# A decoder trunk on one core: held sums copied into PSUM ahead of the last down-projection block, in place of additions after it

## The chip, the core and the metric

The kernel runs on one core of one Trainium2 chip. The metric is device time in microseconds, the median of several runs: 1820.44 us for the kernel before (three runs, 1819.75 to 1821.89). A profile of one execution shows five engines: TensorE (PE, with its weight loads as a row of their own, PEld), VectorE (DVE), ScalarE (ACT), GpSimd (POOL) and SyncE (SP), which starts the transfers.

## What is computed

Two layers of a hybrid decoder, on 512 rows of width 1024, all in float32. Each layer runs a DeltaNet branch and a sliding-window attention branch, merges and projects them (`w_o`), and then an MLP. The part that matters here is the end of a layer:

```python
    x = x + rmsnorm(mix, post_mix_g)

    h2 = rmsnorm(x, pre_mlp_g)
    ff = jnp.square(jax.nn.relu(h2 @ w_ff1)) @ w_ff2
    return x + rmsnorm(ff, post_mlp_g)
```

`ff` is 512 x 1024 and sums over 4096 inner columns. After it come the mean square of each row, a scaling by `post_mlp_g`, the residual sum, and for the first layer the next layer's norm and projection.

## The kernel before

Each float32 product is made of three matmuls: both operands are split into a high part (`h`, rounded to a TensorE format) and a low part (`l`, the rest), and high x high, high x low and low x high go into the same PSUM bank. A weight block `wr` of 128x1024 comes by DMA, ScalarE casts it to `wh` (L384), and VectorE makes `wl` = `wr` - `wh` (L385). Four such pairs are held at once (`LOOK`), and a cast is placed four blocks ahead of its use.

The inner dimension of the MLP goes in four blocks of 1024. The first three down blocks use a Strassen-like scheme with seven products, and their sums are held in eight SBUF tiles `acc[t][n]`: t is one of four row tiles of 128 rows, n one of two column halves of 512. The fourth block (`s = 3`) is plain:

- `ff1` (L1455) makes the last 1024 inner columns in four pairs of units. Each pair uses the banks `ps_a`, `ps_y`, `ps_z` and `ps_q`, 256 columns of each. The two last products of a pair go into `ps_y` and `ps_z`.
- `mm_b4` (L437) makes the first column half of all four row tiles together: for each of four weight blocks j, for each row tile t, six matmuls of 128x512 into the bank `ps_b` of that tile. All four tiles so end within the last block, one after another. Then, for each tile (L1638 to L1641), VectorE adds the held sum `acc[t][0]` to the bank (into SBUF), ScalarE takes the mean square of the sum (L506, `jk`, a junk output with an accumulated row sum), and VectorE multiplies it by the gain.
- `last_tiles` (L424, first layer) makes the second column half, `ps_f`: row tile 0, then 1, with 24 matmuls each, then 2 and 3 in turns of two k. After tile 0, tile 1 and the pair it calls `post_tiles` (L545): VectorE adds the held sum `acc[t][1]` (L560), ScalarE takes its mean square (L506), VectorE multiplies by the gain (L565), joins the mean squares (L511), GpSimd makes the power -1/2 (L512), and VectorE scales both halves and adds the residual (L568, L569). Then come the next layer's mean squares (L506), GpSimd's root, its scaling into `xs` (L521), and TensorE transposes `xs` into banks `ps_n` (L532, eight small matmuls for a row tile, in four-by-four), from which ScalarE and VectorE take the high and low parts (L537, L538). The transposes of tiles 0 and 1 stand between the matmuls of tiles 2 and 3 and those of tiles 2 and 3 between the next layer's first matmuls. In the last layer a plain loop (L1651) makes tile after tile, and the end of `post_tiles` stores to the output.

The eight PSUM banks are dealt to pools: `PM` (two), `PS` (three), `PK` (one), `PZ` (two). In the kernel before, `mm_b4` gets two of `PZ` and two of `PS` (`four(1)`), and `last_tiles` three turns of `PM` and `PK`.

The same function `last_tiles` is used for `w_o` earlier in the layer, where nothing is held: there ScalarE's mean square (L506) and VectorE's gain (L565, and L1366 after `mm_b4`) read the PSUM banks `ps_wo` and `ps_b` directly.

A scheduler sets the order of each engine's instructions outside the stretches that `Order` pins to the order of writing. TensorE's order at the places named here is that of the code. Engines run their queues in order.

Of the kernel before, what the change touches and what calls it, by code (L numbers as in the profile page):

```python
# [15 lines left out]
ALU = mybir.AluOpType  # L16
# [7 lines left out]
NT = S // P  # L24
KT = D // P
# [102 lines left out]
def hybrid_trunk(ctx, tc, x, positions, pre_mix_g, dn_conv_w, dn_a_log, dn_dt_bias, dn_norm_g,  # L128
# [286 lines left out]
    def mm_b(ps, ws, aT, t, ks=range(KT)):  # L415
        tsl = slice(t * P, (t + 1) * P)
        for k in ks:
            hi, lo = aT[k]
            wh, wl = ws[k // 2]
            mm(ps, lhsT=hi[:, tsl], rhs=wh[:, k % 2, :], start=k == 0, stop=False)  # L420
            mm(ps, lhsT=hi[:, tsl], rhs=wl[:, k % 2, :], start=False, stop=False)
            mm(ps, lhsT=lo[:, tsl], rhs=wh[:, k % 2, :], start=False, stop=k == KT - 1)

    def last_tiles(ws, aT, name, done, turn):  # L424

        pss = [PM(name), PM(name), PM(name), PK(name)]
        for t in range(2):
            mm_b(pss[t], ws, aT, t)
            done((t,), pss[t:])
        for k in range(0, KT, 2):  # L430
            for t in (2, 3):
                mm_b(pss[t], ws, aT, t, range(k, k + 2))
            if k in (0, 4):
                turn(k // 4)
        done((2, 3), pss[2:])

    def mm_b4(pss, aT, then=lambda: None):  # L437

        for j in range(4):
            if j == 2:  # L440
                then()
            wh, wl = weights()
            for t in range(NT):
                tsl = slice(t * P, (t + 1) * P)
                for r in range(2):
                    hi, lo = aT[j * 2 + r]
                    k = j * 2 + r
                    mm(pss[t], lhsT=hi[:, tsl], rhs=wh[:, r, :], start=k == 0, stop=False)  # L448
                    mm(pss[t], lhsT=hi[:, tsl], rhs=wl[:, r, :], start=False, stop=False)  # L449
                    mm(pss[t], lhsT=lo[:, tsl], rhs=wh[:, r, :], start=False, stop=k == KT - 1)  # L450

    def mm_c(pss, left, onto=False, js=range(2)):

# [24 lines left out]
    def four(i):  # L478
        return [b("ps_b4") for b in ((PZ, PZ, PS, PS) if i % 2 else (PM, PM, PK, PS))]
# [22 lines left out]
    def meansq(src, name):  # L502

        jk = T[4]("jk", BF16)
        q_ = sm.tile([P, 1], F32, name=name, bufs=5)
        act(out=jk, in_=src, func=AF.Square, scale=D ** -0.5, accum_out=q_)  # L506
        return q_
# [37 lines left out]
    def post_tiles(tiles, a0g, ps1, add1, q0, gb, xsrc, xdst, gb2=None, Tx=(T[5], T[6], T[7])):  # L545
# [12 lines left out]
        if add1 is not None:  # L558
            for i, t in enumerate(tiles):
                tt(out=add1[t], in0=a[i], in1=add1[t], op=ALU.add)  # L560
                a[i] = add1[t]
        q1 = [meansq(a[i], "pq1") for i in n]
        r = []
        for i, t in enumerate(tiles):
            tt(out=xo[i][:, 512:], in0=a[i], in1=gb[:, 512:], op=ALU.mult)  # L565
            r.append(rstd("pr", q0[t], q1[i]))
        for i, t in enumerate(tiles):
            stt(out=xo[i][:, :512], in0=a0g[t], scalar=r[i], in1=xt[i][0], op0=ALU.mult, op1=ALU.add)  # L568
# [26 lines left out]
    for l in range(depth):  # L595
# [778 lines left out]
            dma(xd[t * P:(t + 1) * P, :], xo)  # L1374

        def wo_tail(tiles, pss):
            xs.extend(post_tiles(tiles, m0, pss, None, s0, gb1, x_res, keep, gb2))

        last_tiles(ws, mT, "ps_wo", wo_tail, lambda t: norm_turn(xs[t], t, q2))

# [30 lines left out]
                dma(out[t * P:(t + 1) * P, i * 512:(i + 1) * 512], xo[:, i * 512:(i + 1) * 512])  # L1411

        def ff2_tail(tiles, pss):
            a0, a1 = [a[0] for a in acc], [a[1] for a in acc]
            Tx = T[0], T[3], T[6]
            if l == depth - 1:
                post_tiles(tiles, a0, pss, a1, s0, gb3, xd, give, None, Tx)
            else:
                xs_next.extend(post_tiles(tiles, a0, pss, a1, s0, gb3, xd, keep, nxt[0], Tx))
# [101 lines left out]
        for s in range(3):  # L1521
# [30 lines left out]
            def done(ms, ps):  # L1552
                if len(ms) == 2:
                    raw[ms[0] // 4] = ps
                else:
                    m, = ms
                    if m in (0, 2, 4, 6):
                        raw[m // 4] = X4("raw")
                    r_ = raw[m // 4].rearrange("p (a k n) -> p a k n", a=2, k=2)[:, :, m % 2, :]
                    act(out=r_, in_=ps.rearrange("p (a n) -> p a n", a=2), func=AF.Relu)  # L1560
                    act(out=r_, in_=r_, func=AF.Square)
                count[0] += len(ms)
                if count[0] % 4 == 0:
                    lefts(*raw)
# [68 lines left out]
                      *(a.rearrange("p (a n) -> p a n", a=2) for a in h3[m]))  # L1633

        ff1(done, pending)
        pss = four(1)
        mm_b4(pss, h3)
        for t in range(NT):  # L1638
            tt(out=acc[t][0], in0=pss[t], in1=acc[t][0], op=ALU.add)
            s0[t] = meansq(acc[t][0], "pq0")  # L1640
            tt(out=acc[t][0], in0=acc[t][0], in1=gb3[:, :512], op=ALU.mult)  # L1641
        ws = [weights() for _ in range(4)]
        if l < depth - 1:
            nxt = pre_begin(l + 1)
            xs_next = []
            order = Order(nc.tensor)
            order.begin()
            last_tiles(ws, h3, "ps_f2", ff2_tail, lambda t: norm_turn(xs_next[t], t, nxt[1]))
# [31 lines left out]
```

## Time and profile before

| what | value |
| --- | --- |
| median of three runs | 1820.44 us (1819.75 to 1821.89) |
| the profiled execution's own time | 1820.0 us |
| its span, first to last instruction | 1818.3 us |
| TensorE busy | 1796.3 us, 99% |
| VectorE busy | 1386.4 us, 76% |
| ScalarE busy | 994.9 us, 55% |
| TensorE clock, mean | 0.999 |

A row of the timeline reads: start in us from the span's start, duration in us, engine, line, operation, output <- input with shapes, how many instructions are merged, and in brackets how long the engine had been idle and whose result ended that. Matmuls overlap in their pipeline: a matmul of 128x512 lasts 0.39 us in the records, but the next starts 0.23 us after it.

### The profile page before, as it was taken

Reading aid. Unit: us, or ns where it says so; the run is one execution under the profiler, and the core shown is the slowest. Engines: PE = TensorE matmul, PEld = TensorE weight load, DVE = VectorE, ACT = ScalarE, POOL = GpSimd, SP = SyncE. Lnnn points to the kernel's source line nnn. Section 1 sums busy time; section 2 is a strip of 40 time slices with the busy share of each in tenths; the row PEclk is TensorE's granted clock in tenths of the full one; section 3 lists DMA queues with packets and bytes.
Section 4 is the critical chain, followed back from the end, with each engine's and each line's share of the span. In section 5 each row is a group of like instructions: output and inputs, shape, how many; then the busy total and the mean of one; then the engine's idle time right before and its main releaser. Section 6 shows DMA issues by size and latency. Waiting matters only on the chain.

```text
span 1818.3 us, 28382 instructions
## 1 busy us (share of the span) xinstructions
PE 1796.3 (99%) x10252; PEld 1524.3 (84%) x10252; DVE 1386.4 (76%) x2606; ACT 994.9 (55%) x2031; POOL 209.4 (12%) x386
## 2 busy tenths in 40 slices
PE   9999999999999999999999999999999999999998
PEld 8878878888788888989898887888877888889896
DVE  5499796887666878898556997968875669798974
ACT  6678742444434656566457877234443347566562
POOL 0322102221101000000012221022111010000000
PEclk9999999999999999999999999999999999999999
DMA  6633447654463244554445344585545533554551
GB/s 201 203 111 121 111 145 226 180 170 152 117 200 136 82 162 153 174 182 146 166 155 180 105 128 110 168 230 157 166 140 153 172 116 105 175 166 158 174 176 57
DMA packets 146431, 278.60 MB, mean 153 GB/s; under 512 B 33569, under 2 KB 66657, under 8 KB 146290
## 3 DMA queue, kind: packets, MB, share of 16 engines
q1 hardware_dynamic: 145778, 276.75, 48.9%
q8 instruction: 81, 1.33, 0.3%
q14 instruction: 60, 0.49, 0.1%
q0 software_dynamic: 512, 0.03, 0.0%
HBM read 239.38 MB, written 37.36 MB: 152 GB/s over the span
## 4 chain that ended last, share of the span: by engine, by line
PE 82%; DVE 5%; ACT 5%; DMA 4%; issue 1%; POOL 1%; SPq 1%; DVEq 0%; POOLq 0%; ACTq 0%
PE ps_b L449 3%; PE ps_b L448 3%; PE ps_b L450 3%; PE ps_f L400 2%; PE ps_f L401 2%; PE ps_f L402 2%; PE ps_us L400 2%; PE ps_us L401 2%; PE ps_us L402 2%; PE ps_ud L401 2%; PE ps_ud L402 1%; PE ps_ud L400 1%; PE ps_vp L402 1%; PE ps_vp L400 1%; PE ps_vp L401 1%
## 5 line engine op out<-in xcount | busy, mean ns | idle before, releaser
L384 ACT CAST wh<-wr 128x1024 fp32r<-128x1024 f32 (+2 forms) x368 | 372.5, 1019 | 439.5 <-PE ps_vp L401 59.0
L385 DVE TENSOR_TENSOR wl<-wr,wh 128x1024 fp32r<-128x1024 f32 (+2 forms) x368 | 435.2, 1191 | 177.6 <-ACT wh L384 174.4
L512 POOL TENSOR_TENSOR pr<-pq,pw 128x1 f32<-128x1 f32 x16 | 9.8, 612 | 793.4 <-DVE pq L511 793.4
L448 PE MATMUL ps_b<-wh,h_h 128*128 128x432 f32 (+1 forms) x192 | 71.1, 370 | 0.0
L449 PE MATMUL ps_b<-wl,h_h 128*128 128x432 f32 (+1 forms) x192 | 70.5, 367 | 0.1
L450 PE MATMUL ps_b<-wh,h_l 128*128 128x432 f32 (+1 forms) x192 | 70.3, 366 | 0.0
L400 PE MATMUL ps_f<-g_h,wh 128*128 128x512 f32 x160 | 62.4, 390 | 0.0
L401 PE MATMUL ps_f<-g_l,wh 128*128 128x512 f32 x160 | 62.4, 390 | 0.0
L402 PE MATMUL ps_f<-g_h,wl 128*128 128x512 f32 x160 | 62.2, 389 | 0.0
L401 PE MATMUL ps_qp<-h_l,wh 128*128 128x512 f32 x128 | 54.0, 422 | 0.0
L400 PE MATMUL ps_vp<-h_h,wh 128*128 128x512 f32 x128 | 53.7, 420 | 0.0
L402 PE MATMUL ps_vp<-h_h,wl 128*128 128x512 f32 x128 | 53.7, 419 | 0.0
L985 ACT ACTIVATE M<-M,nm 128x128 f32<-128x128 f32 x128 | 49.9, 391 | 5.9 <-DVE nm L980 5.9
L400 PE MATMUL ps_qp<-h_h,wh 128*128 128x512 f32 x128 | 51.8, 405 | 0.0
L400 PE MATMUL ps_kp<-h_h,wh 128*128 128x512 f32 x128 | 51.6, 403 | 0.0
L402 PE MATMUL ps_qp<-h_h,wl 128*128 128x512 f32 x128 | 51.4, 401 | 0.0
L401 PE MATMUL ps_vp<-h_l,wh 128*128 128x512 f32 x128 | 51.4, 401 | 0.0
L401 PE MATMUL ps_ga<-h_l,wh 128*128 128x512 f32 x128 | 51.0, 398 | 0.0
L400 PE MATMUL ps_gb<-h_h,wh 128*128 128x512 f32 x128 | 51.0, 398 | 0.0
L402 PE MATMUL ps_kp<-h_h,wl 128*128 128x512 f32 x128 | 50.9, 398 | 0.0
L402 PE MATMUL ps_ga<-h_h,wl 128*128 128x512 f32 x128 | 50.7, 396 | 0.0
L343 DVE TENSOR_TENSOR wr<-wr 128x512 f32<-128x512 f32 x72 | 47.4, 685 | 4.3 <-DMA wr<-in_weights_dram 4.1
(432 smaller groups left out, 5922.5 us busy)
## 6 DMA issues: line engine op xcount, KB each, us to landing
wr<-in_weights_dram SPq DMA_DIRECT2D x320, 512.0 KB, 3.7
wr<-in_weights_dram SPq DMA_DIRECT2D x24, 432.0 KB, 4.7
D<-dd SPq DMA_DIRECT2D x32, 256.0 KB, 2.8
xd<-xo SPq DMA_DIRECT2D x12, 512.0 KB
xt<-xd SPq DMA_DIRECT2D x24, 256.0 KB, 4.1
D<-gd SPq DMA_DIRECT2D x16, 256.0 KB, 6.0
dd<-D SPq DMA_DIRECT2D x16, 256.0 KB, 5.9
kkd<-kk SPq DMA_DIRECT2D x16, 256.0 KB, 2.0
```

Source lines behind the costliest of these rows:

```text
L343: tt(out=o_, in0=i0, in1=i1, op=ALU.add)
L384: nc.scalar.copy(wh[:, :w], wr[:, :w])
L385: sub(out=wl[:, :w], in0=wr[:, :w], in1=wh[:, :w].bitcast(F32), op=ALU.subtract)
L400: mm(ps, lhsT=wh[:, k, :], rhs=hi, start=k == 0, stop=False)
L401: mm(ps, lhsT=wh[:, k, :], rhs=lo, start=False, stop=False)
L402: mm(ps, lhsT=wl[:, k, :], rhs=hi, start=False, stop=k == KT - 1)
L448: mm(pss[t], lhsT=hi[:, tsl], rhs=wh[:, r, :], start=k == 0, stop=False)
L449: mm(pss[t], lhsT=hi[:, tsl], rhs=wl[:, r, :], start=False, stop=False)
L450: mm(pss[t], lhsT=lo[:, tsl], rhs=wh[:, r, :], start=False, stop=k == KT - 1)
L512: ptt(out=r, in0=q1, in1=mhalf[:, 0:1], op=ALU.pow)
L985: act(out=M[:, j * P:(j + 1) * P], in_=M[:, j * P:(j + 1) * P], func=AF.Exp, bias=nm[:, j:j + 1], accum_out=den[:, j:j + 1])
```

## The change

In the plain block the bank gets the held sum first. ScalarE copies `acc[t][0]` into each of `mm_b4`'s four banks, and `acc[t][1]` into each of the second half's banks; all matmuls then add onto that (no matmul of the group has `start`). VectorE's eight additions a layer (L1639 and L560 of before) are gone, ScalarE gets eight copies of 128x512 a layer, and the mean squares and gains read the bank in place of SBUF. The banks are dealt otherwise: `mm_b4` takes `PS`, `PS`, `PZ`, `PZ`, and the second half takes `PZ`, `PZ`, `PZ`, `PS` in the first layer and `PZ` for each tile in the last, in place of `PM` and `PK`.

```diff
-    def last_tiles(ws, aT, name, done, turn):
-
-        pss = [PM(name), PM(name), PM(name), PK(name)]
-        for t in range(2):
-            mm_b(pss[t], ws, aT, t)
+    def last_tiles(ws, aT, name, done, turn, seed=None):
+
+
+        pss = [b(name) for b in ((PZ, PZ, PZ, PS) if seed else (PM, PM, PM, PK))]
+        onto = seed is not None
+        for t in range(NT):
+            if onto:
+                nc.scalar.copy(pss[t], seed[t])
+            if t == 2:
+                break
+            mm_b(pss[t], ws, aT, t, onto=onto)
             done((t,), pss[t:])
+        if onto:
+            nc.scalar.copy(pss[3], seed[3])
...
-            mm(ps, lhsT=hi[:, tsl], rhs=wh[:, k % 2, :], start=k == 0, stop=False)
...
+            mm(ps, lhsT=hi[:, tsl], rhs=wh[:, k % 2, :], start=k == 0 and not onto, stop=False,
+               skip_group_check=onto)
...
-        a = list(ps1[:len(tiles)])
-        if add1 is not None:
-            for i, t in enumerate(tiles):
-                tt(out=add1[t], in0=a[i], in1=add1[t], op=ALU.add)
-                a[i] = add1[t]
+        a = ps1[:len(tiles)]
...
-        pss = four(1)
-        mm_b4(pss, h3)
+        pss = [b("ps_b4") for b in (PS, PS, PZ, PZ)]
         for t in range(NT):
-            tt(out=acc[t][0], in0=pss[t], in1=acc[t][0], op=ALU.add)
-            s0[t] = meansq(acc[t][0], "pq0")
-            tt(out=acc[t][0], in0=acc[t][0], in1=gb3[:, :512], op=ALU.mult)
+            nc.scalar.copy(pss[t], acc[t][0])
+        mm_b4(pss, h3, onto=True)
+        for t in range(NT):
+            s0[t] = meansq(pss[t], "pq0")
+            tt(out=acc[t][0], in0=pss[t], in1=gb3[:, :512], op=ALU.mult)
...
-                ps = PM("ps_f2")
-                mm_b(ps, ws, h3, t)
+                ps = PZ("ps_f2")
+                nc.scalar.copy(ps, acc[t][1])
+                mm_b(ps, ws, h3, t, onto=True)
                 ff2_tail((t,), [ps])
```

The order of the matmuls on TensorE is not changed. Where the copies stand in ScalarE's queue is set by the scheduler. The first place is the end of `ff1`, ahead of `mm_b4` in the first layer (`ps_b_9214` to `ps_b_9217` are the banks of row tiles 0 to 3, `ps_f_9388` to `ps_f_9391` those of the second half). Before, ScalarE has there:

```order
L384 CAST wh<-wr 128x1024
L1500 ACTIVATE raw<-ps_a 128x256
L1493 COPY raw<-ps_q 128x256
L384 CAST wh<-wr 128x1024 x2
L1511 ACTIVATE raw<-raw 128x512
L1513 ACTIVATE raw<-ps_z 128x256
L384 CAST wh<-wr 128x1024
L1514 ACTIVATE raw<-raw 128x1024
L486 CAST h_h<-raw 128x512 x2
```

Now it has:

```order
L384 CAST wh<-wr 128x1024
L1510 ACTIVATE raw<-ps_a 128x256
L1503 COPY raw<-ps_q 128x256
L1648 COPY ps_b_9214<-acc 128x512
L1648 COPY ps_b_9215<-acc 128x512
L384 CAST wh<-wr 128x1024 x3
L1521 ACTIVATE raw<-raw 128x512
L1523 ACTIVATE raw<-ps_z 128x256
L1648 COPY ps_b_9217<-acc 128x512
L1524 ACTIVATE raw<-raw 128x1024
L440 COPY ps_f_9391<-acc 128x512
L500 CAST h_h<-raw 128x512 x2
```

The copies into `ps_b_9214`, `ps_b_9215`, `ps_b_9217` and `ps_f_9391` have come in (that into `ps_b_9216` stands a little earlier), and a weight cast (L384) has moved ahead of the two activations on `raw` (L1511 and L1513, which are L1521 and L1523 now).

The second place is the step from `mm_b4` to the second half, again on ScalarE in the first layer (`pq` and `nq` are the mean squares). Before:

```order
L384 CAST wh<-wr 128x1024 x3
L506 ACTIVATE jk,pq_9340<-acc 128x512
L506 ACTIVATE jk,pq_9345<-acc 128x512
L506 ACTIVATE jk,pq_9350<-acc 128x512
L384 CAST wh<-wr 128x1024
L506 ACTIVATE jk,pq_9355<-acc 128x512
L506 ACTIVATE jk,pq_9423<-acc 128x512
L506 ACTIVATE jk,nq_9433<-xo 128x512
```

Now:

```order
L384 CAST wh<-wr 128x1024 x3
L520 ACTIVATE jk,pq_9343<-ps_b_9214 128x512
L520 ACTIVATE jk,pq_9347<-ps_b_9215 128x512
L520 ACTIVATE jk,pq_9351<-ps_b_9216 128x512
L520 ACTIVATE jk,pq_9355<-ps_b_9217 128x512
L384 CAST wh<-wr 128x1024
L434 COPY ps_f_9388<-acc 128x512
L434 COPY ps_f_9389<-acc 128x512
L520 ACTIVATE jk,pq_9423<-ps_f_9388 128x512
L434 COPY ps_f_9390<-acc 128x512
```

The copies into `ps_f_9388` and `ps_f_9389` stand behind the mean squares of all four `ps_b` banks and behind a weight cast, which has moved behind the fourth mean square. `ps_f_9388` is the bank that `ps_b_9216` had, and `ps_f_9389` that of `ps_b_9217`; `ps_f_9390` has the bank of `ps_f_9388`. The last layer has the same order at this step.

More of the change, by code (lines that the diff above doesn't have):

```diff
@@ L413, in mm_a2, with mm_b @@
             mm(ps[:, c], lhsT=wl[:, k, :], rhs=hi[:, c], start=False, stop=k == KT - 1)
-    def mm_b(ps, ws, aT, t, ks=range(KT)):
+    def mm_b(ps, ws, aT, t, ks=range(KT), onto=False):
         tsl = slice(t * P, (t + 1) * P)
@@ L435, in last_tiles, with mm_b4 @@
         done((2, 3), pss[2:])
-    def mm_b4(pss, aT, then=lambda: None):
+    def mm_b4(pss, aT, then=lambda: None, onto=False):
         for j in range(4):
@@ L447, in mm_b4 @@
                     k = j * 2 + r
-                    mm(pss[t], lhsT=hi[:, tsl], rhs=wh[:, r, :], start=k == 0, stop=False)
-                    mm(pss[t], lhsT=hi[:, tsl], rhs=wl[:, r, :], start=False, stop=False)
-                    mm(pss[t], lhsT=lo[:, tsl], rhs=wh[:, r, :], start=False, stop=k == KT - 1)
+                    mm(pss[t], lhsT=hi[:, tsl], rhs=wh[:, r, :], start=k == 0 and not onto, stop=False,
+                       skip_group_check=onto)
+                    mm(pss[t], lhsT=hi[:, tsl], rhs=wl[:, r, :], start=False, stop=False,
+                       skip_group_check=onto)
+                    mm(pss[t], lhsT=lo[:, tsl], rhs=wh[:, r, :], start=False, stop=k == KT - 1,
+                       skip_group_check=onto)
     def mm_c(pss, left, onto=False, js=range(2)):
@@ L1376, in wo_tail @@
         def wo_tail(tiles, pss):
-            xs.extend(post_tiles(tiles, m0, pss, None, s0, gb1, x_res, keep, gb2))
+            xs.extend(post_tiles(tiles, m0, pss, s0, gb1, x_res, keep, gb2))
         last_tiles(ws, mT, "ps_wo", wo_tail, lambda t: norm_turn(xs[t], t, q2))
@@ L1413, in ff2_tail @@
         def ff2_tail(tiles, pss):
-            a0, a1 = [a[0] for a in acc], [a[1] for a in acc]
+            a0 = [a[0] for a in acc]
             Tx = T[0], T[3], T[6]
             if l == depth - 1:
-                post_tiles(tiles, a0, pss, a1, s0, gb3, xd, give, None, Tx)
+                post_tiles(tiles, a0, pss, s0, gb3, xd, give, None, Tx)
             else:
-                xs_next.extend(post_tiles(tiles, a0, pss, a1, s0, gb3, xd, keep, nxt[0], Tx))
+                xs_next.extend(post_tiles(tiles, a0, pss, s0, gb3, xd, keep, nxt[0], Tx))
         half = lambda i: slice(i * 256, (i + 1) * 256)
@@ L1647, in hybrid_trunk @@
             order.begin()
-            last_tiles(ws, h3, "ps_f2", ff2_tail, lambda t: norm_turn(xs_next[t], t, nxt[1]))
+            last_tiles(ws, h3, "ps_f2", ff2_tail, lambda t: norm_turn(xs_next[t], t, nxt[1]),
+                       [a[1] for a in acc])
             hT = nxt
```

10 lines of the change are left out of this document (6 added, 4 removed).

## The prediction

> **What bounds the kernel now.** I read the head of the page first, then TensorE's waits, then the timelines of the two stretches that the change touches in each layer.
>
> ```profile
> span 1818.3 us, 28382 instructions
> PE 1796.3 (99%) x10252; PEld 1524.3 (84%) x10252; DVE 1386.4 (76%) x2606; ACT 994.9 (55%) x2031; POOL 209.4 (12%) x386
> ```
>
> TensorE is busy for 1796.3 of 1818.3 us. VectorE's additions can therefore cost time only where TensorE waits for what comes after them, or after TensorE's last matmul. By the same rows anything that holds TensorE up is paid in full. The first layer's end is the one place among those touched where TensorE waits:
>
> ```profile
> 908.11 1.39 PE L532 MATMUL ps_n<-ident,xs 128*128 128x128 f32 x8
> 909.25 0.47 PE L420 MATMUL ps_f<-wh,h_h 128*128 128x512 f32 x1
> ...
> 911.87 0.39 PE L422 MATMUL ps_f<-wh,h_l 128*128 128x512 f32 x1
> ...
> 920.05 0.35 PE L422 MATMUL ps_b<-wh,h_l 128*128 128x432 f32 x1
> 920.69 1.29 PE L532 MATMUL ps_n<-ident,xs 128*128 128x128 f32 x8 [0.28 <-DVE xs L521]
> 921.74 0.44 PE L420 MATMUL ps_b<-wh,h_h 128*128 128x432 f32 x1
> ...
> 923.00 0.60 PE L532 MATMUL ps_n<-ident,xs 128*128 128x128 f32 x4
> 924.15 0.66 PE L532 MATMUL ps_n<-ident,xs 128*128 128x128 f32 x4 [0.55 <-DVE h_l L538]
> 924.56 0.44 PE L420 MATMUL ps_b<-wh,h_h 128*128 128x432 f32 x1
> ```
>
> The eight transposes of a row tile (`ps_n`) come four and four from two halves of `xs`. Those of tile 1 took 909.25 - 908.11 = 1.14 us until the next matmul. Those of tile 2 began 0.64 us after the matmul before them, whose like follow each other at 0.19 us (41 steps from 911.87 + 0.23 to 920.05), with the scaled rows `xs` late, and took 1.05 us. Those of tile 3 took 924.56 - 923.00 = 1.56 us, with a wait on VectorE's low parts, `h_l`. What they take when nothing is late stands at the same function's use for `w_o`:
>
> ```profile
> 580.69 0.39 PE L422 MATMUL ps_wo<-wh,mT_l 128*128 128x512 f32 x1
> ...
> 588.11 1.04 PE L532 MATMUL ps_n<-ident,xs 128*128 128x128 f32 x8
> 588.90 0.36 PE L411 MATMUL ps_f<-g_h,wh 128*128 128x256 f32 x1
> ```
>
> There it is 588.90 - 588.11 = 0.79 us. So before loses 0.35 + (0.45 + 0.26) + 0.77 = 1.83 us at the first layer's end. The last layer has no such transposes; after its last matmul the chain runs alone.
>
> **The change part by part.**
>
> *The seeds of the first half.* ScalarE's copies into the four `ps_b` banks must be done before TensorE's first matmul on each.
>
> ```profile
> 862.29 0.36 ACT L1493 COPY raw<-ps_q 128x256 f32<-128x256 f32 x1
> 866.35 0.40 PE L448 MATMUL ps_b<-wh,h_h 128*128 128x512 f32 x1
> ```
>
> ```profile
> 866.22 0.63 ACT L1511 ACTIVATE raw<-raw 128x512 f32<-128x512 f32 x1 [0.19 <-DVE raw L1510]
> 866.76 0.36 ACT L1513 ACTIVATE raw<-ps_z 128x256 f32<-128x256 f32 x1
> ```
>
> The copies for tiles 0 and 1 come behind the copy of 862.29, which ends at 862.65. The one for tile 2 stands earlier and pushes ScalarE by one copy, about 0.55 us (as the step from 866.22 to 866.76, for the same 512 columns), so the two end near 862.65 + 0.55 + 2 x 0.55 = 864.3, 2 us ahead of the first matmul at 866.35. The copy for tile 3 must end by 866.35 + 3 x 1.36 = 870.4 (18 matmuls of 0.227 us come first). It stands behind a cast, which must wait for the last `ps_z` matmul (the one just before 866.35) and takes 0.94 us as shown below, and these two activations: 866.4 + 0.94 + 0.54 + 0.36 + 0.6 = 868.8. Cost: nothing, with 1.6 us to spare; if that cover went, the excess would be paid in full, twice. The last pair's high parts come about 1.2 us later; they are read in the last weight block, over 10 us on.
>
> *The seed of the second half, bank by bank.* This is the term that costs. The second half's first bank is one of the two `PZ` banks, which `mm_b4` held to its end: its row tile 2 must be finished, squared by ScalarE and scaled by VectorE before the seed can go in. And in ScalarE's queue the seed stands behind the mean square of tile 3, which waits for `mm_b4`'s very last matmul, and behind a cast. TensorE's next work is all on that bank, so it stands still. Before, `PM` banks had been free for long. The `w_o` stretch has the same row of events (four mean squares from the banks, then a cast), so the length can be read there:
>
> ```profile
> 557.13 0.39 PE L450 MATMUL ps_b<-wh,mT_l 128*128 128x512 f32 x1
> 557.36 0.39 PE L420 MATMUL ps_wo<-wh,mT_h 128*128 128x512 f32 x1
> 557.55 0.60 ACT L506 ACTIVATE jk<-ps_b 128x512 bf16<-128x512 f32 x1 [0.67 <-PE ps_b L450]
> 558.14 1.04 ACT L384 CAST wh<-wr 128x1024 fp32r<-128x1024 f32 x1
> ...
> 572.53 1.03 ACT L384 CAST wh<-wr 128x1024 fp32r<-128x1024 f32 x1
> 573.47 0.62 ACT L506 ACTIVATE jk<-xo 128x512 bf16<-128x512 f32 x1
> ```
>
> The last `ps_b` matmul starts at 557.13, and TensorE's next, unhindered, at 557.36. The mean square of tile 3 starts at 557.55 and the cast at 558.14. A cast frees ScalarE after 573.47 - 572.53 = 0.94 us, so a seed copy would start at 559.08. No copy from SBUF to PSUM stands in the trace; its neighbours are a copy from PSUM to PSUM and an activation that reads SBUF:
>
> ```profile
> L1595 ACT COPY ps_pw<-ps_py x12: 570/570/605, 643.3 to 1704.8; 128x512 f32<-128x512 f32 x12
> L506 ACT ACTIVATE jk<-acc x16: 613/632/632, 885.8 to 1811.9; 128x512 bf16<-128x512 f32 x16
> ```
>
> That bounds it between 0.57 and 0.63 us; I take 0.60, and the copy ends at 559.68. What TensorE needs from there shows where it waited for a copy into a bank:
>
> ```profile
> 1752.46 0.36 ACT L1498 COPY ps_z<-ps_y 128x256 f32<-128x256 f32 x1
> 1752.88 0.39 PE L473 MATMUL ps_z<-n_h,wh 128*128 128x256 f32 x1
> 1753.10 0.28 PE L475 MATMUL ps_z<-n_l,wh 128*128 128x256 f32 x1
> ```
>
> That copy ended at 1752.82 and the matmul started at 1752.88, 0.06 us on; the next then followed after 0.22 us, where matmuls of 256 columns follow at 0.12, half the 0.23 us of 512, so the restart costs 0.10 us. The stall is 559.74 - 557.36 = 2.38 us, with the restart 2.48 us, in each layer: **+4.96 us** (4.9 to 5.0 by the copy's bounds). The other seeds are hidden: that of tile 1 follows at once, under 5.4 us of tile 0's matmuls; that of the third `PZ` turn waits for tile 0's two readers, about 1.4 us after tile 0's end, under 5.4 us of tile 1's. The other queues lose nothing: SP's weight loads are six blocks ahead, and VectorE waits for TensorE anyway.
>
> *VectorE's additions at the first layer's end.* Without them this stretch becomes that of `w_o`, instruction by instruction. There the scaled rows of tile 2 come 6.25 us after the start of the last matmul of tile 3 (580.69):
>
> ```profile
> 586.94 1.42 DVE L521 SCALAR_TENSOR_TENSOR xs<-xo,nr,gb 128x512 f32<-128x512 f32 x2 [0.43 <-POOL nr L512]
> ...
> 590.48 1.88 DVE L538 TENSOR_TENSOR g_l<-ps_n,g_h 128x512 fp32r<-128x512 f32 x3
> ```
>
> Both halves are done 1.42 us later, at +7.67. TensorE needs them after 42 matmuls of the next layer, at 920.05 + 0.19 - 911.87 = +8.37. They are in time, and the 0.71 us of tile 2 go. Tile 1's `xs` were late behind two additions (0.69 us each); without them its 0.35 us go. Tile 3's wait falls with `h_l`, which VectorE takes up when the `xs` of tile 3 are through: 590.48 - 580.69 = +9.8 there, and the first is done by +10.6, while the second four transposes of tile 3, the first that reuse a bank, come at about 8.37 + 0.79 + 1.2 + 0.4 = +10.8. So all 1.83 us can come back. At worst the wait of this kind that the `w_o` stretch still has stays, about 0.4 us, because one `PS` bank now holds a row tile. I take **-1.7 us**, with -1.4 and -1.83 as ends. The first half's four additions and the others hide under matmuls: nothing.
>
> *The end of the program.* Here the addition stands first after the last matmul, and yet little is gained:
>
> ```profile
> 1810.69 0.39 PE L422 MATMUL ps_f<-wh,h_l 128*128 128x512 f32 x1
> 1811.12 0.69 DVE L560 TENSOR_TENSOR acc<-ps_f,acc 128x512 f32<-128x512 f32 x1 [1.59 <-PE ps_f L422]
> 1811.85 0.69 DVE L565 TENSOR_TENSOR xo<-acc,gb 128x512 f32<-128x512 f32 x1
> ...
> 1813.56 0.75 DVE L568 SCALAR_TENSOR_TENSOR xo<-acc,pr,xt 128x512 f32<-128x512 f32 x1 [0.72 <-POOL pr L512]
> ```
>
> ```profile
> 1811.93 0.63 ACT L506 ACTIVATE jk<-acc 128x512 bf16<-128x512 f32 x1 [4.71 <-DVE acc L560]
> ```
>
> The mean square of the sum (ScalarE) and the gain (VectorE) run side by side from SBUF, at 1811.93 and 1811.85. On a bank they do not, as `w_o` shows (VectorE and ScalarE in turn):
>
> ```profile
> 563.77 0.69 DVE L565 TENSOR_TENSOR xo<-ps_wo,gb 128x512 f32<-128x512 f32 x1 [3.34 <-ACT jk L506]
> ...
> 565.24 0.75 DVE L568 SCALAR_TENSOR_TENSOR xo<-mix,pr,xt 128x512 f32<-128x512 f32 x1 [0.70 <-POOL pr L512]
> ```
>
> ```profile
> 563.05 0.60 ACT L506 ACTIVATE jk<-ps_wo 128x512 bf16<-128x512 f32 x1 [3.88 <-PE ps_wo L422]
> ```
>
> VectorE begins 0.72 us after ScalarE, for about as long as its addition took. From ScalarE's start to the scaled row it is 565.24 - 563.05 = 2.19 us, and ScalarE starts 557.55 - 557.13 = 0.42 us (0.48 for `ps_wo`) after the start of the last matmul. Now it is 1813.56 - 1810.69 = 2.87 us; then 0.45 + 2.19 = 2.64. Gain: **-0.2 us**. The Trainium skill (PSUM — Partial Sum Buffer, section "PSUM bank collisions raise a hardware error") says that two engines must never touch one bank at the same time, two reads included, so that software has to keep them apart. The rows agree: side by side from SBUF, in turn from a bank. Were it not so, the end would gain about 0.9 us, and the sum would be 0.7 us lower.
>
> *Sum:* 4.96 - 1.7 - 0.2 = +3.06 us. Against the profiled execution's own 1820.0 us (1.7 outside its span) that is 1823.1; the median before is 0.44 above it, which gives **1823.5 us**, 0.17% more. A measurement of this kernel can tell about 0.2%, 3.6 us, from no change, that is 1816.8 to 1824.1. With the ends of the terms and about 0.5 us for the medians this case alone spans 1822.5 to 1824.5.
>
> **The rivals.**
>
> *The waits of the first layer's end stay (slower).* The sixth bank of the transposes is the price: `ps_f_9391` takes one of three `PS` banks, which before served the transposes alone. If the transposes of tile 1 or 3 must then wait for the low parts of tile 0 or 2 each time, the 1.7 us do not come back: +4.8 us, 1825.2, and up to 1 us more if the waits grow. It decides from 0.6 us of the 1.7 lost, which puts the sum over 3.6. For it: the 0.55 us on `h_l` in the rows above. Against it: that low part is begun over 1 us earlier relative to TensorE.
>
> *The clock falls in the stall (slower).* A row tells what a long pause does:
>
> ```profile
> 1812.00:1818.30 6.30, 0.00 (x0) 0.00 (x0) 2.11 (x4) 0.65 (x2) 0.54 (x1) 0.65 0.22 83
> ```
>
> In these 6.3 us without matmuls the granted clock averages 0.65, while with the waits above, up to 0.55 us, the mean over the span is 0.999. A pause of 2.4 us lies between. If the clock halved afterwards for about 3 us, each stall would cost 1.5 us more: +6 us, 1826.5. By the Trainium skill (TensorE: Matmul & The Clock Gate, section "Part 1: The HAM clock gate") the clock is cut after an idle window of about 3.4 us, and this stall is shorter; by that rule the sum stands.
>
> *The stall is not there (faster).* If the seed found its bank free, because the readers of `ps_b` are done early or ScalarE does it before the cast, only the gains are left: -1.9 us, 1818.5, within 0.2%. Against it: the order of ScalarE's queue, and that tile 3's mean square cannot start before `mm_b4` ends. Without the cast alone, 0.94 us less a layer: +1.2. To pass 3.6 us below, nothing in the rows suffices unless VectorE's relief counts elsewhere.
>
> **How the numbers follow.** The forecast has 0.72, and reaches past 3.6 us in about a quarter of it. The waits that stay have 0.12, the clock 0.06, no stall or a shorter one 0.07, something faster still 0.03. Slower by over 0.2%: 0.18 + 0.18 = 0.36; faster by over 0.2%: 0.03; within: 0.61. The range takes in the forecast's own span, the shorter stall and most of the waits that stay, and leaves out the clock's case, that without any stall and what is faster still (0.16, with the edges about 0.2): 1821.0 to 1825.6.
>
> **What would show it.** In the changed profile: TensorE's waits should name the seed copy on ScalarE before `ps_f`, twice, 2.3 to 2.5 us each, and none before `ps_b`. The transposes at the first layer's end should take near 0.8 us for each row tile, with waits under 0.5 us in all. From the start of the last matmul to the last scaling's start should be 2.6 to 2.7 us. The mean clock should stay at 0.999. I am wrong if the wait on the seed is under 1.5 us or over 3, if waits on `h_l` or `xs` over 1 us are left, or if seeds of the first half are waited for.

## The result and the profile after

| what | before | after |
| --- | --- | --- |
| median of 17 runs each | 1822.17 us (1817.87 to 1825.08) | 1826.73 us (1824.05 to 1830.00) |
| ratio, after to before | | 1.0026 (95%: 1.0019 to 1.0032) |
| the profiled execution's own time | 1820.0 us | 1827.09 us |
| its span | 1818.3 us | 1825.4 us |
| TensorE clock, mean | 0.999 | 0.997 |

The change makes the kernel slower by 0.26%, 4.6 us (3.5 to 5.8 by the interval). The forecast was +3.06 us, and 1826.73 lies above its range of 1821.0 to 1825.6. The forecast was made against 1820.44 us, and in these runs the kernel before itself stands at 1822.17, which is 1.7 us of the distance between 1823.5 and 1826.73; the other 1.5 us are the change's own.

The head of the page, then TensorE's waits (line waited for: us in total, times, longest):

```profile
span 1825.4 us, 28382 instructions
PE 1797.8 (98%) x10252; PEld 1526.1 (84%) x10252; DVE 1375.9 (75%) x2590; ACT 1002.9 (55%) x2047; POOL 213.1 (12%) x386
```

```profile
PE ps_f L420 <- ACT ps_f L1665: 2.2, 1, 2.2
PE ps_f L420 <- ACT ps_f L434: 2.2, 1, 2.2
```

VectorE lost 10.5 us of work, and TensorE got two new waits, one in each layer, on the seed copy ahead of `ps_f`. None on a copy is listed ahead of `ps_b`. ScalarE's timeline at this place in the first layer, and TensorE's:

```profile
887.91 0.60 ACT L520 ACTIVATE jk<-ps_b 128x512 bf16<-128x512 f32 x1 [0.67 <-PE ps_b L463]
...
888.50 1.03 ACT L384 CAST wh<-wr 128x1024 fp32r<-128x1024 f32 x1
889.43 1.11 ACT L434 COPY ps_f<-acc 128x512 f32<-128x512 f32 x2
```

```profile
887.48 0.39 PE L463 MATMUL ps_b<-wh,h_l 128*128 128x512 f32 x1
890.07 0.50 PE L420 MATMUL ps_f<-wh,h_h 128*128 128x512 f32 x1 [2.20 <-ACT ps_f L434]
...
890.77 0.63 PE L424 MATMUL ps_f<-wh,h_l 128*128 128x512 f32 x1
...
893.33 0.63 PE L424 MATMUL ps_f<-wh,h_l 128*128 128x512 f32 x1
893.75 0.46 PE L420 MATMUL ps_f<-wh,h_h 128*128 128x512 f32 x1
```

Mean square of tile 3, cast, copy: the queue that was forecast, and TensorE restarts at 890.07 where it would have gone on at 887.48 + 0.23, a stall of 2.36 us. What the forecast gave a chance of 0.06 stands behind it. From 890.77 to 893.33 the six steps are 0.43 us each and not 0.23. The table of stretches gives the granted clock (the third number from the end):

```profile
891.00:893.50 2.50, 2.50 (x7) 1.93 (x7) 0.00 (x0) 0.00 (x0) 0.00 (x0) 0.50 0.65 176
...
1795.60:1798.20 2.60, 2.60 (x7) 2.02 (x7) 0.00 (x0) 0.00 (x0) 0.00 (x0) 0.50 0.00 0
...
887.00:890.00 3.00, 0.87 (x4) 0.38 (x2) 1.82 (x3) 2.33 (x7) 0.00 (x0) 1.00 0.18 71
```

In the stall itself the clock is still 1.00; once the matmuls are back it is halved, in both layers (called a fall below). The trace's own record of the granted clock dates the two falls: 890.48 to 893.89 and 1795.01 to 1798.42 us, 3.41 us each. Now the first layer's end, TensorE:

```profile
911.75 1.04 PE L546 MATMUL ps_n<-ident,xs 128*128 128x128 f32 x8
912.54 0.47 PE L420 MATMUL ps_f<-wh,h_h 128*128 128x512 f32 x1
...
923.52 1.03 PE L546 MATMUL ps_n<-ident,xs 128*128 128x128 f32 x8
924.32 0.44 PE L420 MATMUL ps_b<-wh,h_h 128*128 128x432 f32 x1
...
925.57 0.60 PE L546 MATMUL ps_n<-ident,xs 128*128 128x128 f32 x4
926.77 0.66 PE L546 MATMUL ps_n<-ident,xs 128*128 128x128 f32 x4 [0.60 <-DVE h_l L552]
927.18 0.44 PE L420 MATMUL ps_b<-wh,h_h 128*128 128x432 f32 x1
```

Tiles 1 and 2 take 0.79 and 0.80 us, as forecast. Tile 3 takes 927.18 - 925.57 = 1.61 us, no less than before. ScalarE and VectorE there:

```profile
925.00 0.51 ACT L725 COPY qt<-ps_b 128x416 f32<-128x416 f32 x1 [4.38 <-DVE ba L724]
925.40 1.57 ACT L551 CAST h_h<-ps_n 128x512 fp32r<-128x512 f32 x3
```

```profile
923.46 1.42 DVE L535 SCALAR_TENSOR_TENSOR xs<-xo,nr,gb 128x512 f32<-128x512 f32 x2 [0.72 <-POOL nr L526]
924.79 0.17 DVE L724 COPY ba<-ps_b 128x16 f32<-128x16 f32 x1
926.03 1.29 DVE L552 TENSOR_TENSOR h_l<-ps_n,h_h 128x512 fp32r<-128x512 f32 x2 [1.06 <-ACT h_h L551]
```

The high parts of tile 2 (`h_h`), ready to be cast since about 924.2 (0.67 us after their transposes began, as in the kernel before), stand behind the copy of `qt`, which waits for VectorE's small copy `ba`, which stands behind the scaled rows of tile 3. In the kernel before, two of these casts were ahead of `qt`.

The program's end, all engines:

```profile
1817.94 0.39 PE L424 MATMUL ps_f<-wh,h_l 128*128 128x512 f32 x1
1818.45 0.60 ACT L520 ACTIVATE jk<-ps_f 128x512 bf16<-128x512 f32 x1 [4.75 <-PE ps_f L424]
...
1819.17 0.69 DVE L575 TENSOR_TENSOR xo<-ps_f,gb 128x512 f32<-128x512 f32 x1 [2.54 <-ACT jk L520]
...
1820.65 0.75 DVE L578 SCALAR_TENSOR_TENSOR xo<-acc,pr,xt 128x512 f32<-128x512 f32 x1 [0.72 <-POOL pr L526]
```

It is 2.71 us from the last matmul to the last scaling, against 2.87.

### The profile page after: what moved, and what is told of

Read it like the earlier page. It is cut to its first block, busy times and chain, and to the rows that moved or that the text cites. A ratio compares the mean times of both kernels' runs of the same rounds, so it can differ in the third digit from the quotient of the medians.

```text
span 1825.4 us, 28382 instructions
## 1 busy us (share of the span) xinstructions
PE 1797.8 (98%) x10252; PEld 1526.1 (84%) x10252; DVE 1375.9 (75%) x2590; ACT 1002.9 (55%) x2047; POOL 213.1 (12%) x386
## 4 chain that ended last, share of the span: by engine, by line
PE 86%; DVE 4%; ACT 4%; DMA 3%; issue 1%; SPq 1%; POOL 1%; DVEq 0%; POOLq 0%; ACTq 0%
PE ps_b L459 3%; PE ps_b L461 3%; PE ps_b L463 3%; PE ps_f L400 2%; PE ps_f L401 2%; PE ps_f L402 2%; PE ps_us L400 2%; PE ps_us L401 2%; PE ps_us L402 2%; PE ps_ud L401 2%; PE ps_ud L402 1%; PE ps_ud L400 1%; PE ps_vp L402 1%; PE ps_vp L400 1%; PE ps_qp L401 1%; PE ps_qp L400 1%
## 5 line engine op out<-in xcount | busy, mean ns | idle before, releaser
L384 ACT CAST wh<-wr 128x1024 fp32r<-128x1024 f32 (+2 forms) x368 | 372.7, 1019 | 433.8 <-PE ps_vp L401 60.1
L401 PE MATMUL ps_gb<-h_l,wh 128*128 128x512 f32 x128 | 50.6, 395 | 0.0
```

The lines of the kernel that those rows point to most:

```text
L384: nc.scalar.copy(wh[:, :w], wr[:, :w])
L401: mm(ps, lhsT=wh[:, k, :], rhs=lo, start=False, stop=False)
```

## The experiments

The theory after this reading: two stalls on the seed copy, a clock that halves behind them by chance, and a give-back that one order on ScalarE cuts short. The rivals stand in each expectation. Every ratio is to runs of the kernel before on the same chip beside it (medians 1819.5 us for e1 to e4, 1818.9 for e5 to e8, 1819.5 for e9 and e10). In the diffs, `-` is the changed kernel unless another is named.

**Only the first half seeded (e1_first_half).** The second half is as in the kernel before.

```diff
     def post_tiles(..., ps1, add1, ...):
+            for i, t in enumerate(tiles):
+                tt(out=add1[t], in0=a[i], in1=add1[t], op=ALU.add)
...
-            last_tiles(ws, h3, "ps_f2", ff2_tail, ..., [a[1] for a in acc])
+            last_tiles(ws, h3, "ps_f2", ff2_tail, ...)
...
-                ps = PZ("ps_f2")
-                nc.scalar.copy(ps, acc[t][1])
-                mm_b(ps, ws, h3, t, onto=True)
+                ps = PM("ps_f2")
+                mm_b(ps, ws, h3, t)
```

> Only the first column half is seeded; the second half is as in the kernel before (own banks, VectorE adds the held sum). Theory (all of the loss comes from the seed copy that TensorE waits for ahead of the second half, and from the clock after it): no wait on a copy ahead of `ps_f`, the clock stays at .999, and the time is that of the kernel before within 1 us (1821 to 1823, with 1822.2 for before). Rival (the first half's seeds cost too, because ScalarE has eight more copies or the banks of `mm_b4` are held longer): 2 us or more above before with no stall at `ps_f`.

Measured: 1819.20 us, ratio 0.9999 (0.9991 to 1.0008). No wait ahead of `ps_f`; the transposes take 1.13, 1.05 and 1.56 us, as before. The first half's four copies in each layer neither cost nor gain anything that shows; the interval leaves room for about 1.6 us either way.

**Only the second half seeded, on an early bank (e2_second_half).**

```diff
-        pss = [b("ps_b4") for b in (PS, PS, PZ, PZ)]
+        pss = four(1)
+        mm_b4(pss, h3)
         for t in range(NT):
-            nc.scalar.copy(pss[t], acc[t][0])
-        mm_b4(pss, h3, onto=True)
-        for t in range(NT):
-            s0[t] = meansq(pss[t], "pq0")
-            tt(out=acc[t][0], in0=pss[t], in1=gb3[:, :512], op=ALU.mult)
+            tt(out=acc[t][0], in0=pss[t], in1=acc[t][0], op=ALU.add)
+            s0[t] = meansq(acc[t][0], "pq0")
+            tt(out=acc[t][0], in0=acc[t][0], in1=gb3[:, :512], op=ALU.mult)
```

> Only the second half is seeded, and its first bank is the one that held row tile 0 of the first half, whose readers are done 4 us before the half ends. Theory (the stall is the chain from the end of `mm_b4` through the readers of a bank to the copy, not the copy itself): TensorE steps from the first half to the second in under 0.3 us, the clock stays at .999, and only the gains are left, about -1.0 us at the first layer's end and -0.2 us at the program's end: 1821.0, from 1820.3 to 1821.7 with 1822.2 for before. Rival (a seed copied by ScalarE is late wherever its bank is, since ScalarE's queue is behind): a wait of 1 us or more on the copy ahead of `ps_f`, and 1824 or more.

Measured: 1817.19 us, ratio 0.9991 (0.9982 to 1.0000). TensorE steps over in 0.23 us; the transposes take 0.79, 0.79 and 1.61 us. From the last `ps_b` matmul of the first half to the end of tile 3's transposes it is 921.99 - 886.39 = 35.60 us, against 924.56 - 887.91 = 36.65 before: -1.05 us. A seed copied by ScalarE is not late as such.

**Work in the stall (e3_fill).** Sixteen transposes of no use between the halves.

```diff
+        order = Order(nc.tensor)
+        order.begin()
+        fill = PM("ps_fill")
+        for _ in range(16):
+            tr(fill[:, 0:P], ident, ident)
+        order.end()
         ws = [weights() for _ in range(4)]
```

> The changed kernel with 16 small transposes into an unused bank on TensorE between the first half and the second, in each layer; they compute nothing that is used. They lie where TensorE stood still. Theory (the clock falls because TensorE pauses): the first matmul on `ps_f` still starts about 2.4 us after the last one of `mm_b4` would have let it, but the matmuls behind it follow at 0.23 us at once, the clock is .998 or better in every run, and the time is 3.5 us above before, 1825.7 (1824.9 to 1826.5), with no run over 1827.5. Rival (the slow matmuls after the wait have another cause, such as weights that come late or the bank's first accumulation): the same steps of 0.43 us and the same time as the changed kernel, 1826.7, with runs up to 1830.

Measured: 1821.28 us, ratio 1.0012 (1.0003 to 1.0021), which is 2.2 us above before (0.5 to 3.8), with 0.999 for the clock in all 11 runs. TensorE in the first layer, then its stretch behind the restart:

```profile
887.00 0.39 PE L463 MATMUL ps_b<-wh,h_l 128*128 128x512 f32 x1
887.23 1.91 PE L1654 MATMUL ps_fill<-ident 128*128 128x128 f32 x16
889.60 0.50 PE L420 MATMUL ps_f<-wh,h_h 128*128 128x512 f32 x1 [0.46 <-ACT ps_f L434]
```

```profile
890.50:893.00 2.50, 2.50 (x13) 2.05 (x12) 0.00 (x0) 0.00 (x0) 0.00 (x0) 1.00 0.59 174
```

The first `ps_f` matmul is as late as in the changed kernel (2.37 us), on the same copy into the same bank, and the clock stays at 1.00. So it is the pause that halves the clock, not the copy or the accumulation onto it. From the start of the first `ps_f` matmul to that of the last it is 23.47 us in the first layer (889.60 to 913.07) and 21.67 in the last (1789.54 to 1811.21), where the changed kernel had 25.07 (890.07 to 915.14) and 23.29 (1794.65 to 1817.94): the falls cost 1.60 and 1.62 us. The stretches of this trace add up to +3.8 us, at the upper end of the interval; the +3.5 (2.7 to 4.3) that was expected is above the +2.2 measured, and the distance is open. One run was over 1825 us (1825.73), with the clock at 0.999.

**The first half's banks dealt otherwise (e4_banks).**

```diff
-        pss = [b("ps_b4") for b in (PS, PS, PZ, PZ)]
+        pss = [b("ps_b4") for b in (PZ, PS, PS, PZ)]
```

> The changed kernel with one thing dealt otherwise: `mm_b4` takes the banks PZ, PS, PS, PZ in place of PS, PS, PZ, PZ, so that the second half's first bank is that of row tile 0 and not of row tile 2. Theory (the bank's last readers make the stall): no wait on the copy ahead of `ps_f` over 0.3 us, no fall of the clock, and the gains alone: 1821.0 (1820.3 to 1821.8), that is 5 to 6 us below the changed kernel. Rival (the copies or the additional accumulation cost by themselves): 1824 or more although no wait is seen there.

Measured: 1819.05 us, ratio 0.9993 (0.9985 to 1.0002). ScalarE, then TensorE:

```profile
886.62 0.60 ACT L520 ACTIVATE jk<-ps_b 128x512 bf16<-128x512 f32 x1 [0.67 <-PE ps_b L463]
...
887.21 0.59 ACT L434 COPY ps_f<-acc 128x512 f32<-128x512 f32 x1
887.98 0.60 ACT L520 ACTIVATE jk<-ps_b 128x512 bf16<-128x512 f32 x1 [0.18 <-PE ps_b L463]
```

```profile
888.91 0.39 PE L463 MATMUL ps_b<-wh,h_l 128*128 128x512 f32 x1
889.14 0.39 PE L420 MATMUL ps_f<-wh,h_h 128*128 128x512 f32 x1
```

The copy now stands between the mean squares of tiles 1 and 2 and ends before 887.98, over a microsecond ahead of TensorE. Stall and fall are both gone, and the `ps_f` matmuls take 23.33 us (889.14 to 912.47), 0.14 less than in e3_fill, which is the price of a restart. All 16 copies of the change are still there, and no loss is left: it came from one choice of banks, with the place in ScalarE's queue that goes with it. The median fell 0.5 us, the ratio says -1.3 (-2.7 to +0.4), and the same stretch as above is 35.60 us, 1.05 less than before.

**Pauses of many lengths (e5_ladder).** In the kernel before, ahead of each product that makes an activation tile from a whole weight block (what the pause computes is overwritten):

```diff
     def mm_a(ps, aT, ks=range(KT), w=None):
         wh, wl = w = w or weights()
+        if 0 in ks:
+            n = site[0] % 7 + 1
+            site[0] += 1
+            tr(ps[:, 0:P], ident, ident)
+            for i in range(n):
+                nc.scalar.copy(gap, ps[:, 0:P] if i == 0 else gap)
+            tr(ps[:, 0:P], gap, ident)
```

> The kernel before with a pause put ahead of each product that makes an activation tile from a whole weight block: a transpose into its bank, a chain of 1 to 7 small ScalarE copies of it in turn, a transpose of the result, then the product as before (which starts the bank anew, so nothing of this is used). It gives many pauses of TensorE of about 0.5 to 4 us within one execution, followed by matmuls of one size. Theory (a pause of about 2.4 us can halve the clock, by where it falls in some window): after pauses under about 1.5 us no matmul step is 0.43 us; between about 1.7 and 3.4 us some pauses have such steps behind them for about 3 us and others none; over 3.5 us all have. Rival (a pause has to fill 3.4 us; the slow steps of the changed kernel have to do with the copy into the bank or what follows it): no slow steps after any pause under 3.4 us.

Measured: one execution, 2145.33 us, mean clock 0.955. TensorE at three of the pauses, and below them the stretches behind each:

```profile
302.37 0.33 PE L408 MATMUL ps_us<-ident,gap 128*128 128x128 f32 x1 [2.30 <-ACT gap L407]
...
443.07 0.33 PE L408 MATMUL ps_qp<-ident,gap 128*128 128x128 f32 x1 [1.80 <-ACT gap L407]
...
443.95 0.63 PE L411 MATMUL ps_qp<-h_h,wh 128*128 128x512 f32 x1
...
1646.47 0.33 PE L408 MATMUL ps_zp<-ident,gap 128*128 128x128 f32 x1 [1.63 <-ACT gap L407]
```

```profile
302.30:307.00 4.70, 4.63 (x21) 3.88 (x22) 4.70 (x21) 0.02 (x1) 0.00 (x0) 1.00 0.31 112
1646.40:1650.00 3.60, 3.53 (x16) 2.94 (x17) 3.03 (x4) 0.42 (x2) 0.00 (x0) 1.00 0.58 107
443.90:447.30 3.40, 3.40 (x9) 2.64 (x8) 3.25 (x9) 1.14 (x2) 1.36 (x2) 0.50 0.12 39
```

The pause of 1.63 us leaves the clock at 1.00; 1.80 us halves it 0.9 us later, for 3.4 us; 2.30 us does not at this place. Counted over the pauses of the ladder that stand alone (no other idle time over 0.2 us within 4.5 us before or 5 us after):

| pause | number | clock halved behind it |
| --- | --- | --- |
| 0.29 to 1.77 us | 21 | 0 |
| 1.80 to 2.53 us | 9 | 8 |
| 2.72 to 3.81 us | 11 | 10 |

So for these pauses there is an edge between 1.77 and 1.80 us, and above it some pauses are spared. The theory held: none under 1.5 us halved it, between 1.7 and 3.4 us some did and others (2.30, 3.33) did not, and the one over 3.5 us (3.81) did. The rival of 3.4 us fell.

Which pauses are spared is not chance, as the trace's record of the granted clock shows. All its 88 entries in this execution lie on one raster, with marks 3.413 us apart, and so do those of each of the changed kernel's two traces (1795.01 lies 265 marks behind 890.48). Where the raster lies differs from execution to execution. What counts at a mark is for how much of the stretch just over, the 3.41 us since the mark before, TensorE stood idle. The stretch ahead of the first fall in the changed kernel, then the two stretches of the ladder that share its pause of 3.33 us (800.52 to 803.84):

```profile
887.07:890.48 3.41, 1.21 (x6) 0.71 (x5) 2.30 (x3) 2.74 (x7) 0.00 (x0) 1.00 0.12 50
```

```profile
798.90:802.31 3.41, 1.62 (x8) 1.06 (x6) 1.61 (x2) 2.44 (x5) 0.00 (x0) 1.00 0.47 154
802.31:805.72 3.41, 1.88 (x9) 1.59 (x10) 3.31 (x5) 1.35 (x5) 0.00 (x0) 1.00 0.00 0
```

In the first, 3.41 - 1.21 = 2.20 us were idle, 64%, and the clock fell at its end. A mark cut the pause of 3.33 us in two, with 52% and 45% of the two stretches idle, and the clock stayed. Of all 569 stretches of the ladder at full clock, it was halved behind all 33 that were idle for more than 54%, behind 9 of 18 between 45 and 54%, and behind 2 of 518 under 45%.

Pauses that follow each other closely add up: one of 0.74 and one of 1.21 us with a single small transpose between them, at 321 to 324 us, halved it too. Two single waits of 1.10 and 1.23 us elsewhere (102 and 90 us) also had halved steps behind them, the 2 of 518 (37% and 40% idle); there the matmuls ahead are small ones of another section, and what they add was not tried.

**The casts ahead of the `qt` copy (e6_casts_first).** On top of e4_banks:

```diff
                 nc.scalar.copy(qt[t][:, 0:416], ps[:, 16:NB])
+                if l > 0:
+                    tc.add_manual_dep(..., casts[2].name, ..., reason="order")
```

> The kernel of e4_banks, and in the second layer's start the first copy of `qt` on ScalarE is held behind the two casts of `h_h` of row tile 2, as it stood in the kernel before. Theory (tile 3's transposes wait because those casts stand behind that copy, which waits for VectorE): the transposes of tile 3 take 0.8 us in place of 1.6, no wait on `h_l` over 0.3 us, and the time is 0.8 us below e4_banks, 2.0 us below before (1.2 to 2.8). Rival (the wait is for a bank, since the second half holds one of three): 1.6 us again and the time of e4_banks.

Measured: 1818.03 us, ratio 0.9994 (0.9985 to 1.0003). TensorE, then ScalarE:

```profile
919.28 1.03 PE L546 MATMUL ps_n<-ident,xs 128*128 128x128 f32 x8
921.33 1.03 PE L546 MATMUL ps_n<-ident,xs 128*128 128x128 f32 x8
```

```profile
919.92 1.08 ACT L553 CAST h_h<-ps_n 128x512 fp32r<-128x512 f32 x2 [3.54 <-PE ps_n L546]
920.88 0.53 ACT L728 COPY qt<-ps_b 128x416 f32<-128x416 f32 x1
```

The transposes of tile 3 are one row of eight without a wait, 0.79 us; the stretch is 922.12 - 887.34 = 34.78 us, 1.87 less than before. That shows the cause of the lost 0.8 us: an order on ScalarE, not a bank. In the median of the whole kernel these 0.8 us are not told from nothing.

**The cast behind the copy (e7_cast_behind).** The changed kernel, with the first seed copy of the second half written ahead of the second half's weights and their casts held behind it:

```diff
+        early0 = [PZ("ps_f2")]
+        nc.scalar.copy(early0[0], acc[0][1])
+        copied = nc.cur_bb.bb.instructions[-1]
...
+                tc.add_manual_dep(i, copied.name, ..., reason="order")
```

> The changed kernel with the weight cast that stands ahead of the first seed copy of the second half put behind it on ScalarE; banks as in the changed kernel. Theory (mean square, cast and copy add up to the stall): TensorE stands still for 2.36 - 0.94 = 1.42 us in each layer. A pause of this length should not halve the clock, so the mean clock is .999 and the time is 2 x (1.42 + 0.12) - 1.16 = 1.9 us above before (1.0 to 2.8). Rival for the clock (any pause of over 1 us on a bank that is copied into halves it): steps of 0.43 us behind it in some runs, and 4 to 5 us above before. Rival for the chain (the bank's reader on VectorE comes later than the cast): a stall of 2.0 us or more still.

Measured: 1821.13 us, ratio 1.0012 (1.0003 to 1.0021), that is +2.2 us; the clock is at 0.999 or 1.000 in all 11 runs. ScalarE, then TensorE:

```profile
887.73 0.60 ACT L520 ACTIVATE jk<-ps_b 128x512 bf16<-128x512 f32 x1 [0.67 <-PE ps_b L463]
...
888.32 0.59 ACT L1654 COPY ps_f<-acc 128x512 f32<-128x512 f32 x1
888.83 1.04 ACT L384 CAST wh<-wr 128x1024 fp32r<-128x1024 f32 x1
```

```profile
887.31 0.39 PE L463 MATMUL ps_b<-wh,h_l 128*128 128x512 f32 x1
888.96 0.50 PE L420 MATMUL ps_f<-wh,h_h 128*128 128x512 f32 x1 [1.26 <-ACT ps_f L1654]
```

The stall is 888.96 - 887.31 - 0.23 = 1.42 us, as worked out from the chain, and its 1.26 us of idle time are 37% of a stretch at most: no fall.

**The changed kernel again (e8_after_again).** No edit.

> The changed kernel itself, beside the others on this chip, for the spread of its clock. Theory (the clock halves behind none, one or both of the two pauses, by chance): its runs list mean clocks of .999, .998 and .997, each step of .001 about 1.8 us longer, and those at .999 are about 3.5 us above before. Rival (the clock of this kernel is lower throughout): one clock value in all runs.

Measured: 1826.97 us over 5 runs, ratio 1.0036 (1.0024 to 1.0049). With the 17 runs above, by the mean clock that each lists:

| mean clock | the 17 runs above | these runs |
| --- | --- | --- |
| 0.999 | 4 runs, mean 1824.6 us | 1 run, 1822.0 |
| 0.998 | 5 runs, mean 1825.8 us | 3 runs, mean 1826.3 |
| 0.997 | 8 runs, mean 1827.8 us | 1 run, 1827.0 |

The two profiled executions, both 0.997, have two falls. If 0.998 is read as one and 0.999 as none, which no trace shows, there were 16 + 5 + 2 + 3 = 26 falls behind 44 stalls. The count is rough: the six kernels without a stall (e1, e2, e4, e6, e9, e10) also list 0.998 in 4 of their 66 runs. The four runs at 0.999 among the 17 lie about 2.9 us above the mean of its runs before (1821.7), near the forecast's sum.

**Both remedies on the second half alone (e9_half_casts), and e6 once more (e10_casts_again).** e9 is e2_second_half with the edit of e6; e10 is e6 without any edit.

> The two remedies on the half that pays: only the second column half is seeded, its first bank is the one of row tile 0 (e2_second_half), and the first copy of `qt` in the second layer is held behind the casts of `h_h` of row tile 2 (e6_casts_first). Theory: transposes of 0.8 us for each row tile, no wait on a seed copy, time 2.0 us below before (ratio .9989, from .9985 to .9994). Rival (the gain in the stage is lost elsewhere in the program): a ratio of 1.000 although the stage is 1.9 us shorter.

> The kernel of e6_casts_first once more, with both halves seeded, to narrow its interval and to set it beside e9_half_casts on one chip. Theory: the first half's seeds cost and gain nothing, so it is within 0.5 us of e9_half_casts, 2.0 us below before (ratio .9985 to .9994). Rival: the four more copies on ScalarE in each layer cost 1 us or more, and it is slower than e9_half_casts by that.

Measured: 1817.89 us, ratio 0.9992 (0.9983 to 1.0001), and 1817.78 us, ratio 0.9996 (0.9987 to 1.0005), a little above the 0.9985 to 0.9994 that was expected. In both traces the stretch is 34.78 us. The five kernels with a seeded second half and no stall (e2, e4, e6, e9, e10) have ratios from 0.9991 to 0.9996, mean 0.9993, 1.2 us below before, and each interval reaches 1. That they beat the kernel before by the 1.2 to 2.0 us that their stages show is likely and not settled; that they beat the changed kernel, at 1.0026 and 1.0036, is.

## Why the prediction was wrong

Term by term, in the profiled execution:

| term | forecast | trace of after |
| --- | --- | --- |
| seeds of the first half | 0 | 0 |
| two stalls, with the restart | +4.96 | 2 x (2.36 + 0.14) = +5.0 |
| clock behind the stalls | 0 | 1.60 + 1.62 = +3.2 |
| give-back at the first layer's end | -1.7 | -1.05 |
| end of the program | -0.2 | -0.16 |
| sum | +3.06 | +7.0 (span: +7.1) |

In the rest of the program the two traces differ by -0.43 us ahead of the first stall (887.48 against 887.91 us) and by +0.51 between the two stretches. That these cancel, and the sum meets the span so closely, is luck.

- **Right:** that nothing waits ahead of `ps_b`; that the seed copy, behind a mean square and a cast, stops TensorE in both layers, and for how long. The chain read off at `w_o` gave 2.38 us and 2.36 came. The copy itself took 0.59 us (0.60 taken). Mean square and gain on one bank ran in turn, and the end gained what that leaves.
- **Wrong, the step that decides:** "The mean clock should stay at 0.999." The rival "the clock falls in the stall" was written down, and its price of 1.5 us was near the 1.6 measured; its chance of 0.06 was the mistake, and with it the term of 0. It rested on a rule: the Trainium skill (TensorE: Matmul & The Clock Gate, section "Part 1: The HAM clock gate") has the cut come after an idle window of about 3.4 us. The trace disagrees: 2.2 us of idle time was enough here, and 1.80 in the ladder, since about half of a 3.41 us stretch suffices. The row that was quoted beside it said as much. With a mean clock of 0.65 over the 6.3 us from 1812.00, full at first and halved then, the fall comes after 1.9 us, at 1813.9, which is 2.8 us after the last matmul ended (1810.69 + 0.39). It was read as a pause of 6.3 us, and the fall in it was not dated. The 0.55 us below and those 2.8 us above left 2.4 open; 0.06 was not open.
- **Wrong in size:** the give-back. The forecast had "all 1.83 us can come back" and put the low end at -1.4; it was -1.05. The step that failed is that this stretch "becomes that of `w_o`, instruction by instruction". It does not on ScalarE: the copy of `qt`, which `w_o` has not, had moved ahead of the `h_h` casts. The order of the changed kernel was read at the two places where the seeds stand, and not here. With the casts ahead again (e6) -1.87 came.
- **The rival "the waits of the first layer's end stay"** came true by half: 0.8 us of them stayed, but not because a bank was lacking.

It took two things to carry the median out of the range: the change's own +4.6 us and the 1.7 us by which the kernel before stood higher in these runs, for which, with all else about the medians, the forecast had allowed about 0.5 us. Set on 1820.44 the +4.6 would give 1825.0, inside the range, and the forecast's +3.06 set on 1822.17 would give 1825.2, inside too. An estimate from the 26 falls behind 44 stalls puts the clock at 1.9 us of the +4.6 (26 x 1.6 us over 22 runs); without it the median would be about 1824.8, inside as well. Without both falls the terms of the trace give +3.8 us.

## What to carry to other kernels

A copy that seeds a PSUM bank cost nothing here that showed; which bank it goes into decided, since it must wait for that bank's last readers and for whatever stands ahead of it in its engine's queue. Give the first accumulation of a stage the bank whose old tile ends first, and read the queue of the copying engine up to there. And price a new pause of TensorE twice: by its length, and, once it can fill about half of a 3.41 us stretch (1.7 us and more), by a stretch at half the clock behind it.

## What the runs showed of the hardware that was not expected

- The granted clock changes only at marks 3.41 us apart, and is halved where about half or more of the stretch just over was idle (in the ladder 33 of 33 stretches idle for more than 54%, 9 of 18 between 45 and 54%, 2 of 518 under 45%). A single pause of 1.77 us or less did not do it in 21 cases; a longer one does it by where it lies on the raster (18 of 20 in the ladder; by the runs' mean clocks, roughly, 26 of 44 in the changed kernel).
- A fall starts up to 1.4 us after the matmuls are back, lasts 3.41 us (in 12 of the ladder's 44 cases twice that), and costs about 1.6 us.
- The Trainium skill (the same section) has a window of 3.4 us that runs on by itself. The raster agrees with that. An estimate from that page's window: with half of it idle as the rule, the edge would lie at 1.7 us, and a stall with 2.20 us of idle time would be caught in 2.20 / 3.4 = 65% of cases. The ladder's edge and the 26 of 44 (59%) agree roughly with that; why the stretches between 45 and 54% go either way was not shown.
- Sixteen small transposes in a pause of 2.37 us kept the mean clock at 0.999 in all 11 runs, and a gap of 0.46 us between them and the next matmul did no harm.
